# A ConvFFN whose weight-block sums move to VectorE, with reordered tile steps and an open last tile

## The chip, the cores and the metric

The kernel runs on one core of a Trainium2 chip. The metric is device time in microseconds (us), from the start to the end of one execution. Three runs of the kernel before gave 2868.24, 2868.50 and 2880.14 us; the median is 2868.5 us. A core has five engines, each with an instruction queue of its own that it works through in order: TensorE (PE in the profile; its weight loads are PEld), VectorE (DVE), ScalarE (ACT), GpSimd (POOL) and SyncE (SP), which here issues DMA transfers. Results of matmuls go to PSUM banks; everything else lies in SBUF.

## The reference

The program is a backbone of two layers on 1024 latent tokens and 256 context tokens, with a model width of 1024. Layer 0 mixes tokens by a Fourier transform and a gated unit, layer 1 by neighbourhood attention. Each layer ends in a ConvFFN, which is what the change is about:

```
def conv_ffn(h, w_up, conv_w, conv_b, w_down):
    a = h @ w_up                                  # w_up: 1024 x 5632
    gate, val = a[..., :D_FF], a[..., D_FF:]      # D_FF = 2816
    g = gate[t-1]*conv_w[0] + gate[t]*conv_w[1] + gate[t+1]*conv_w[2] + conv_b
    return (silu(g) * val) @ w_down               # w_down: 2816 x 1024
x = x + g2 * conv_ffn(modulate(x, ...), ...)      # latents, both layers
ctx = ctx + cg2 * conv_ffn(modulate(ctx, ...), ...)   # context, layer 0 only
```

Layer 1 is the last one, so its ConvFFN works on the latents alone, that of layer 0 on latents and context. All data is 32-bit; the kernel gets the accuracy by splitting an operand into a high part (a rounded copy, on ACT) and a low part (the difference, on DVE) and using three matmuls (high by high, high by low, low by high).

## The kernel before, in words

**Tiles and passes.** A ConvFFN runs two passes, one for each half of the tokens (L470 `run`). In a pass, a loop goes over 22 tiles of 128 gate and 128 value columns of `w_up`. In layer 1 a half is 2 x 256 or 2 x 258 tokens, in layer 0 it is 2 x 320 or 2 x 324.

**Products.** Each tile's up projection is a 2x2 block product (gate and value columns times the two parts of the token half, with the depth of 1024 cut in two) done in seven products instead of eight, in the manner of Strassen and Winograd. The weights' operands are the blocks A00, A01, A11 and the sums S1 to S4: `S1 = A10 + A11` ("s", L270), `S3 = A00 - A10` (L279), `S2 = S1 - A00` (L280), `S4 = A01 - S2` (L283). The tokens' operands are B00, B10, B11 and the sums T1, T2, T3, N4. Products P1 to P7 are 12 matmuls each (L352). P6, P7, P4 and P3 continue in PSUM banks of earlier products, so between two of them the running sum is copied out: "c00" after P1, "U" after P6, "V" after P7, "c10" after P4, all copies on ACT (L366). The adds "c00+", "c11+", "c01+" are on DVE (L363).

**The weights' way.** `load0` and `load1` (L265) bring two blocks of 512 KB each into the two `wr` buffers, by SP. A `wr` buffer is free for the next load only when the low part of the last operand made from it is done. POOL makes the four sums; ACT makes the high parts (L273), DVE the low parts (L277). S3, S2 and S4 overwrite the raw blocks, so low A00 comes before S3 and S2, and low S1 before S4.

**The rest of a tile.** "gate" (L370, ACT) and "taps" (L377 and L379, DVE) are the convolution; then "silu" (L397, ACT), "mul" (L398, DVE), and the split of the result into `act`: "acth" (L384, ACT) and "actl" (L388, DVE). In the token lists a minus sign marks a step that belongs to the tile before. Down projection steps D0 to D3 (L428) use two finished tiles each, and their results are taken into the residual by X0 to X3 (L420, DVE). "prep" fetches a block of `w_down` (L295) and splits an earlier one (L550 on ACT, L551 on DVE). "N" runs one step of the `ahead` generator, which in pass 0 prepares the token operands of pass 1 on DVE and ACT and sends them to a buffer in HBM.

**What sets the order.** The lists STEADY, START (tile 0 of pass 0), SECOND (tile 1) and TURN (between the passes) hold the steps of one tile in program order; every engine gets its own instructions in that order. A wait therefore holds up whatever stands behind it on the same engine.

**Ends and entries.** START is fed by `operands` (L222), which makes the seven token operands of half 0 for each of four depth blocks in turn, with subtractions at L246. At the end of pass 1 the down projection of the last six feed-forward tiles stands alone (L515 on): first output blocks 4 to 7 for tiles NF-4 and NF-3 with a take each, then for each half of the tokens all eight output blocks for the last two tiles. In layer 1 each finished block is transposed (L1806), copied (L1810) and sent out (L1813). The attention stage starts with transposes of `vt` (L1161), whose context part is copied by DVE (L1155).

Of the kernel before, what the change touches and what calls it, by code (L numbers as in the profile page):

```python
# [78 lines left out]
class Ffn:  # L79
# [89 lines left out]
    def ahead(self):  # L169
# [52 lines left out]
    def operands(self):  # L222
# [3 lines left out]
        n = h.n  # L226
        self.late = {}
        x = {j: (self.hf[j][:, :n], self.hf[j][:, n:2 * n], self.hf[j + 4][:, :n], self.hf[j + 4][:, n:2 * n]) for j in range(4)}

        def split(op, j, x):  # L230
            self.net.split(self.part(0, op, j, 0), self.part(0, op, j, 1), x)
        for j in range(4):
            for i, c in enumerate(h.kept):
                if j < 3:
                    nc.scalar.activation(self.halo[:, j::4, i], self.hfa[j][:, :, c:c + 4], AF.Copy)
                else:
                    for k in (j, j + 4):
                        nc.scalar.activation(self.halo[:, k, i], self.hf[k][:, c:c + 4], AF.Copy)
            split("B00", j, x[j][0])
        for op, i in (("B10", 2), ("B11", 3)):  # L240
            for j in range(4):
                split(op, j, x[j][i])
        for j in range(4):
            b00, b01, b10, b11 = x[j]
            for o, a, b in ((b00, b01, b00), (b01, b11, b01), (b11, b11, b00), (b10, b10, b11)):
                nc.vector.tensor_tensor(o, a, b, ALU.subtract)  # L246
            for op, o in (("T1", b00), ("T2", b11), ("T3", b01), ("N4", b10)):
                if op == "T1" and j < 2:
                    split(op, j, o)
                else:  # L250
                    self.late.setdefault(op, []).append(lambda op=op, j=j, o=o: split(op, j, o))


    def up_weights(self, f, slots):
# [4 lines left out]
        op = nc.gpsimd.tensor_tensor  # L259
# [55 lines left out]
    def up(self, s, f, norm):  # L315
# [154 lines left out]
    def run(self, hooks, beside, early, done):  # L470
# [59 lines left out]


class Net:
# [243 lines left out]
    def finish(self, mats, srcs, order, update, ffn, acc, square):  # L776
# [349 lines left out]
    def qkv(self, h, pool, ready, begun):  # L1126
# [24 lines left out]
        def vv(pr, pl, pc):  # L1151
# [3 lines left out]
            nc.vector.tensor_copy(vt[:, NL:], pc)  # L1155
# [345 lines left out]
    def run(self, out):  # L1501
# [179 lines left out]
        with pool(name="psb", bufs=2, space=PSUM) as self.ps:  # L1681
# [32 lines left out]
            def done(d, b):  # L1714
                o, c = room(d, b), 0
# [3 lines left out]
                if 0 < d < KD - 1:  # L1719
# [49 lines left out]
        with pool(name="psd", bufs=2, space=PSUM, reuse_waits="tile") as self.ps, pool(name="ffn1", bufs=1) as fp:  # L1769
# [51 lines left out]
            def done(d, b):  # L1821
                if d > 0:
                    emit(d - 1, *((384, 256), (640, 384))[b])
                if d == KD - 1:
# [69 lines left out]
```

## Time and profile before

| What | Value |
| --- | --- |
| Median of three runs | 2868.5 us |
| The profiled execution's own time | 2875.23 us |
| Span in the profile | 2873.4 us |
| Busy: PE, DVE, ACT, POOL | 2759.1, 2241.9, 1399.4, 774.7 us |
| ConvFFN of layer 0, pass 0 and pass 1 | about 486 to 960, and 960 to 1370 us |
| qkv and attention | about 1392 to 2030 us |
| ConvFFN of layer 1, pass 0 and pass 1 | about 2098 to 2505, and 2505 to 2850 us |

The stage bounds are read from the first and last instructions of the lines of a stage. A row of a timeline gives the start of an instruction, its duration, the engine, the line and what it reads and writes; the bracket at the end is the idle time of the engine before it, and what ended that. A row of groups gives busy time, the mean of one in ns, and the sum of the idle times before them. A row of windows gives, for a stretch of time, the busy time of PE, PEld, DVE, ACT and POOL, then the clock granted to TensorE (1.00 is full speed), the share of the DMA engines and GB/s.

### The profile page before, as it was taken

What the parts mean: (1) busy time and instruction counts of PE and PEld (TensorE: products, weight loads), DVE (VectorE), ACT (ScalarE), POOL (GpSimd) and SP (SyncE); (2) the same over time, 40 slices, a digit from 0 to 9 for tenths busy, and PEclk for the clock granted to TensorE, in tenths of its full rate; (3) what the DMA queues carried; (4) which work ended last, traced back from release to release, by engine and by line L of the source; (5) the groups of instructions that cost most, each with busy time, mean ns of one, the idle gap of its engine ahead of it and who ended that gap; (6) DMA issues with size and microseconds to landing.
All of it is one profiled execution on the core that took longest, in us unless ns stands there. A gap on an engine that the chain in (4) does not pass through costs nothing.

```text
span 2873.4 us, 47178 instructions
## 1 busy us (share of the span) xinstructions
PE 2759.1 (96%) x17980; PEld 2516.1 (88%) x17980; DVE 2241.9 (78%) x3746; ACT 1399.4 (49%) x2784; POOL 774.7 (27%) x704
## 2 busy tenths in 40 slices
PE   7999998999999999999899998999989999999999
PEld 4668877999999999999788887999778889899998
DVE  4233477899999888888775676998279999999996
ACT  4322314554445544444443335998255555555554
POOL 0600013232222332222211111444323333243331
PEclk9999999899999999999799999999989999999999
DMA  8764262223334222222043325774223333433333
GB/s 290 215 198 136 79 213 90 89 86 98 96 96 146 83 81 82 81 81 82 14 139 140 131 102 165 182 179 113 59 59 103 113 107 105 133 98 105 92 104 96
DMA packets 347291, 334.79 MB, mean 117 GB/s; under 512 B 14825, under 2 KB 280121, under 8 KB 347065
## 3 DMA queue, kind: packets, MB, share of 16 engines
q1 hardware_dynamic: 342917, 322.85, 37.5%
q0 software_dynamic: 3808, 7.87, 0.9%
q8 instruction: 142, 2.33, 0.3%
q10 hardware_dynamic: 340, 1.06, 0.1%
q14 instruction: 84, 0.69, 0.1%
HBM read 281.43 MB, written 50.29 MB: 115 GB/s over the span
## 4 chain that ended last, share of the span: by engine, by line
PE 64%; DVE 21%; ACT 6%; issue 4%; DMA 3%; POOL 0%; SPq 0%; POOLq 0%; DVEq 0%; ACTq 0%
PE pq L352 19%; PE pq L581 15%; PE pq L428 11%; PE ps L581 6%; DVE xl L420 4%; DVE wh L277 3%; DVE wq L277 3%; DVE wd L551 3%; PE pq L669 2%; PE ps L590 2%; DVE g L377 2%; DVE g L398 2%; DMA wd<-in_ada_w_dram 1%; ACT g L370 1%; PE st L1305 1%
## 5 line engine op out<-in xcount | busy, mean ns | idle before, releaser
L428 PE MATMUL pq<-act,wd 128*128 128x320 f32 (+3 forms) x3696 | 611.0, 317 | 5.6 <-ACT act L384 4.9
L352 PE MATMUL pq<-hs,wh 128*128 128x320 f32 (+3 forms) x4128 | 599.0, 298 | 11.3 <-ACT hx L366 7.4
L352 PEld LDWEIGHTS pq<-hs,wh 128*128 128x128 f32 x4128 | 573.2, 190 | 17.7 <-ACT hx L366 9.4
L428 PEld LDWEIGHTS pq<-act,wd 128*128 128x128 f32 x3696 | 548.6, 190 | 25.6 <-ACT act L384 5.4
L352 PE MATMUL pq<-hs,wq 128*128 128x320 f32 (+3 forms) x3144 | 477.1, 301 | 37.6 <-ACT hx L366 34.7
L352 PEld LDWEIGHTS pq<-hs,wq 128*128 128x128 f32 x3144 | 441.7, 191 | 52.1 <-ACT hx L366 46.6
L581 PE MATMUL pq<-hs,wh 128*128 128x512 f32 (+3 forms) x2100 | 469.0, 358 | 3.3 <-DVE hs L823 3.3
L581 PEld LDWEIGHTS pq<-hs,wh 128*128 128x128 f32 x2100 | 365.8, 192 | 77.4 <-issue 6.2
L270 POOL TENSOR_TENSOR ws<-wr 128x512 f32<-128x512 f32 x88 | 131.6, 1496 | 734.0 <-DMA wr<-in_ffn_w_up_dram 537.9
L420 DVE SCALAR_TENSOR_TENSOR xl<-pq,mod,xl 128x320 f32<-128x320 f32 (+5 forms) x604 | 288.7, 510 | 15.1 <-PE pq L428 15.1
L366 ACT ACTIVATE hx<-pq 128x320 f32<-128x320 f32 (+3 forms) x352 | 143.8, 409 | 301.1 <-PE pq L352 277.7
L277 DVE TENSOR_TENSOR wq<-wr,wq 128x512 fp32r<-128x512 f32 x262 | 240.5, 937 | 25.1 <-ACT wq L273 24.9
L581 PE MATMUL ps<-hs,wh 128*128 128x512 f32 x840 | 242.5, 408 | 4.2 <-ACT hs L820 1.7
L280 POOL TENSOR_TENSOR wr<-ws,wr 128x512 f32<-128x512 f32 x88 | 117.4, 1334 | 260.2 <-DVE wh L277 241.0
L581 PEld LDWEIGHTS ps<-hs,wh 128*128 128x128 f32 x840 | 143.4, 193 | 42.8 <-issue 14.4
L273 ACT ACTIVATE wh<-ws 128x512 fp32r<-128x512 f32 x172 | 108.0, 628 | 148.2 <-PE pq L352 145.3
L277 DVE TENSOR_TENSOR wh<-ws,wh 128x512 fp32r<-128x512 f32 x172 | 157.3, 914 | 21.7 <-ACT wh L273 19.3
L273 ACT ACTIVATE wq<-wr 128x512 fp32r<-128x512 f32 x262 | 162.9, 622 | 17.8 <-POOL wr L279 11.6
L1105 DVE RECIPROCAL hsq<-hsq 128x512 f32<-128x512 f32 (+1 forms) x40 | 121.1, 3030 | 52.8 <-ACT hsq L1104 51.9
L363 DVE TENSOR_TENSOR hx<-hx,pq 128x320 f32<-128x320 f32 (+3 forms) x266 | 118.6, 446 | 42.2 <-PE pq L352 26.0
L551 DVE TENSOR_TENSOR wd<-wrd,wd 128x512 fp32r<-128x512 f32 x176 | 142.6, 849 | 0.0
L279 POOL TENSOR_TENSOR wr<-wr,wr 128x512 f32<-128x512 f32 x88 | 135.7, 1542 | 6.9
(321 smaller groups left out, 4229.1 us busy)
## 6 DMA issues: line engine op xcount, KB each, us to landing
wr<-in_ffn_w_up_dram SPq DMA_DIRECT2D x176, 512.0 KB, 4.5
wrd<-in_ffn_w_down_dram SPq DMA_DIRECT2D x88, 512.0 KB, 3.6
adaw<-in_ada_w_dram SPq DMA_DIRECT2D x128, 256.0 KB, 3.6
wd<-in_ada_w_dram SPq DMA_DIRECT2D x32, 512.0 KB, 4.7
wr<-in_odd_w_qkv_dram SPq DMA_DIRECT2D x24, 512.0 KB, 4.2
vd<-kvs SPq DMA_DIRECT2D x8, 1280.0 KB, 7.3
v<-vd SPq DMA_DIRECT2D x16, 640.0 KB
kd<-kvs SPq DMA_DIRECT2D x8, 1280.0 KB, 4.6
```

Of the source, the lines that this page charges most:

```text
L270: op(raw["S1"], raw["A10"], raw["A11"], ALU.add)
L273: nc.scalar.activation(slots[name][:, 0], raw[name], AF.Copy)
L277: nc.vector.tensor_tensor(slots[name][:, 1], x, f32(slots[name][:, 0]), ALU.subtract)
L279: op(raw["A10"], x, raw["A10"], ALU.subtract)
L352: nc.tensor.matmul(o, w[wn][:, wp, k], self.part(s, bn, k, sp), start=(onto is None and k == 0 and i == 0), stop=(k == 3 and i == 2), skip ...
L363: return lambda: nc.vector.tensor_tensor(x[o], x[a], x[b], ALU.add)
L366: return lambda: nc.scalar.activation(x[o], x[a], AF.Copy)
L420: nc.vector.scalar_tensor_tensor(x, pd[:, a - lo:b - lo], net.mod[:, self.layer, st, 5, d:d + 1], x, ALU.mult, ALU.add)
L428: self.nc.tensor.matmul(pd, self.wds[j][i][:, wp, d % 4], self.acts[f][:, sp, lo:lo + m], start=(first and pi == 0), stop=(last and pi == 2))
L551: return (e or self.nc.vector).tensor_tensor(l, src, f32(h), ALU.subtract)
L581: nc.tensor.matmul(o, w(wp, k), s(k, sp), start=(ki == 0 and pi == 0), stop=(ki == len(order) - 1 and pi == 2))
L1105: nc.vector.reciprocal(r, r)
```

## The change

The change has five parts.

1. The four sums of weight blocks of each tile are made by VectorE instead of GpSimd (the one line in `up_weights`).
2. In STEADY the copy "U" stands ahead of "acth-", "prep" comes after "mul-" instead of ahead of P2, and "N" stands in the list twice, with `ahead` cut into smaller steps.
3. The entry (START, SECOND and `operands`) makes the token operands one operand at a time and not one depth block at a time, and its products come in another order (P1+ and P2+, the second depth halves, ahead of P3).
4. At the end of pass 1, output blocks 4 to 7 of tiles NF-4 and NF-3 stay open in eight PSUM banks and are finished with the last two tiles, so that they are taken once and not twice. The blocks then come in the order 4, 5, 6, 7, 0, 1, 2, 3, and one early transposed output stands behind every second of them.
5. The context part of `vt` is copied by ACT, and the last pair of heads has its products in the order k, q, v.

```
-    STEADY = ("P1", "X2-", "prep", "P2", "c00", "silu-", "mul-", "hA00", "P6", "acth-", "c00+", "actl-", "P5", "U", "hA01",
+    STEADY = ("P1", "X2-", "P2", "c00", "silu-", "mul-", "prep", "hA00", "P6", "c00+", "U", "acth-", "P5", "actl-", "hA01",
               "lA00", "X3-", "P7", "hS1", "lS1", "D0", "V", "c11+", "lA01", "P4", "hS2", "hS3", "X0", "lS2", "D1", "c10",
-              "lS3", "load0", "hA11", "P3", "lA11", "load1", "X1", "N", "D2", "hS4", "c01+", "gate", "lS4", "taps", "D3", "s")
+              "lS3", "N", "load0", "hA11", "P3", "lA11", "load1", "X1", "N", "D2", "hS4", "c01+", "gate", "lS4", "taps", "D3", "s")
-    START = ("P1", "first", "hA00", "lA00", "oT1", "P2", "c00", "hA01", "lA01", "c00+", "P3", "oT2", "sums", "P1+", "oT3",
-             "hS1", "lS1", "c00++", "P2+", "c00p+", "P5", "oN4", "hS2", "lS2", "prep", "P6", "U", "load0", "c01+", "P7", "V",
-             "c11+", "hS3", "lS3", "c01p5", "P4", "c10", "hA11", "lA11", "gate", "load1", "hS4", "taps", "lS4", "s")
-    SECOND = ("P6", "silu-", "hA00", "U", "mul-", "P5", "acth-", "hA01", "lA00", "actl-", "P7", "hS1", "lS1", "V", "c11+",
+    START = ("P1", "first", "hA00", "lA00", "oB11", "P2", "c00", "hA01", "lA01", "c00+", "P1+", "dT1", "oT1", "P2+", "dT3",
+             "sums", "P3", "dT2", "oT2", "c00++", "P5", "oT3", "hS1", "lS1", "P6", "U", "c00p+", "c01+", "dN4", "oN4",
+             "P7", "V", "hS2", "lS2", "c11+", "load0", "hS3", "lS3", "c01p5", "P4", "c10", "gate", "hA11", "lA11", "taps",
+             "load1", "hS4", "prep", "lS4", "s")
+    SECOND = ("P6", "U", "silu-", "hA00", "mul-", "P5", "acth-", "hA01", "lA00", "actl-", "P7", "hS1", "lS1", "V", "c11+",
...
     def up_weights(self, f, slots):
-        op = nc.gpsimd.tensor_tensor
+        op = nc.vector.tensor_tensor
...
     def run(self, hooks, beside, early, done):
...
-        side = early()
-        for d in range(4, KD):
-            self.down(1, NF - 3, d)
-            next(side, None)
-        self.prep(NF)
+        side, out = early(), {}
+        for i in range(2):
+            for d in range(4, KD):
+                if i == 0:
+                    out[d] = self.outs(1)
+                self.down_part(NF - 3, i, d, out[d], i == 0, False)
+                if d % 2:
+                    next(side, None)
+            self.down_weights(NF - 1, (i,))
         for b, block in enumerate(self.blocks(1)):
-            for d in range(KD):
-                self.down(1, NF - 2 + d // 4, d, [block])
-                if d == 0:
+            for n, d in enumerate((4, 5, 6, 7, 0, 1, 2, 3)):
+                if d < 4:
+                    self.down(1, NF - 2, d, [block])
+                else:
+                    for i in range(2):
+                        self.down_part(NF - 1, i, d, out[d][b:b + 1], False, i == 1)
+                    self.take(1, d, out[d][b:b + 1])
+                if n == 0:
                     for _ in side:
                         pass
-                done(d, b)
+                done(n, d, b)
...
-            nc.vector.tensor_copy(vt[:, NL:], pc)
+            nc.scalar.activation(vt[:, NL:], pc, AF.Copy)
...
-            for which in range(3):
+            for which in (1, 0, 2) if pr == NPAIR - 1 else range(3):
```

The first place is VectorE in a steady tile of layer 1, pass 1, from the last low parts of one tile's weights (`wq`) to the product by the value columns (`g<-g,hx`). `xl` rows are takes, the two rows with `cols` are the taps, `wd` rows are the low parts of `w_down`. Before:

```order
L277 TENSOR_TENSOR wq_20845<-wr_27941,wq_20845 128x512
L420 SCALAR_TENSOR_TENSOR xl_3681<-pq_28108,mod_127,xl_3681 128x256
L420 SCALAR_TENSOR_TENSOR xl_3681<-pq_28115,mod_127,xl_3681 128x258
L363 TENSOR_TENSOR hx_27982<-hx_27982,pq_28039 128x258
L277 TENSOR_TENSOR wh_20648<-ws_27980,wh_20648 128x512
L377 SCALAR_TENSOR_TENSOR g_28160<-hx_27982,cols_175_786,g_28160 128x515
L379 SCALAR_TENSOR_TENSOR g_28160<-hx_27982,cols_175_786,g_28160 128x515
L420 SCALAR_TENSOR_TENSOR xl_3783<-pq_28144,mod_127,xl_3783 128x256
L420 SCALAR_TENSOR_TENSOR xl_3783<-pq_28151,mod_127,xl_3783 128x258
L551 TENSOR_TENSOR wd_28197<-wrd_28004,wd_28197 128x512
L551 TENSOR_TENSOR wd_28200<-wrd_28004,wd_28200 128x512
L398 TENSOR_TENSOR g_28160<-g_28160,hx_27982 128x516
```

After (the line numbers are those of the changed kernel):

```order
L284 TENSOR_TENSOR wq_20797<-wr_27921,wq_20797 128x512
L428 SCALAR_TENSOR_TENSOR xl_3681<-pq_28088,mod_127,xl_3681 128x256
L428 SCALAR_TENSOR_TENSOR xl_3681<-pq_28095,mod_127,xl_3681 128x258
L371 TENSOR_TENSOR hx_27962<-hx_27962,pq_28019 128x258
L284 TENSOR_TENSOR wh_20628<-ws_27960,wh_20628 128x512
L385 SCALAR_TENSOR_TENSOR g_28140<-hx_27962,cols_175_786,g_28140 128x515
L387 SCALAR_TENSOR_TENSOR g_28140<-hx_27962,cols_175_786,g_28140 128x515
L277 TENSOR_TENSOR ws_28159<-wr_28120 128x512
L428 SCALAR_TENSOR_TENSOR xl_3783<-pq_28124,mod_127,xl_3783 128x256
L428 SCALAR_TENSOR_TENSOR xl_3783<-pq_28131,mod_127,xl_3783 128x258
L406 TENSOR_TENSOR g_28140<-g_28140,hx_27962 128x516
L568 TENSOR_TENSOR wd_28193<-wrd_28000,wd_28193 128x512
```

The sum S1 (`ws<-wr`) now stands on VectorE behind the taps and ahead of two takes and of the product `g<-g,hx`, which has moved ahead of the `wd` rows. The transfer that S1 reads is issued when the first row of the piece is done.

The second place is ScalarE in the same tile: from the gate (`g<-hx,cols,cols`) to the high part of `act`. `hx<-pq` rows are the copies c00 and U, `wh` rows are high parts of weights. Before:

```order
L370 ACTIVATE g_27563<-hx_27385,cols_31_139,cols_175_786 128x516
L550 ACTIVATE wd_27600<-wrd_27407 128x512
L550 ACTIVATE wd_27603<-wrd_27407 128x512
L366 ACTIVATE hx_27584<-pq_27585 128x258
L397 ACTIVATE g_27563<-g_27563 128x516
L273 ACTIVATE wh_20647<-wr_27527 128x512
L384 ACTIVATE act_27637<-g_27563 128x516
L366 ACTIVATE hx_27584<-pq_27585 128x258
```

After:

```order
L378 ACTIVATE g_27543<-hx_27365,cols_31_139,cols_175_786 128x516
L374 ACTIVATE hx_27564<-pq_27565 128x258
L405 ACTIVATE g_27543<-g_27543 128x516
L567 ACTIVATE wd_27596<-wrd_27403 128x512
L567 ACTIVATE wd_27599<-wrd_27403 128x512
L280 ACTIVATE wh_20627<-wr_27507 128x512
L374 ACTIVATE hx_27564<-pq_27565 128x258
L392 ACTIVATE act_27619<-g_27543 128x516
```

U is now ahead of the high part of `act`, which waits for VectorE's product, and the two `wd` rows are behind silu.

The third place is VectorE at the entry of layer 0's ConvFFN, from its first low part of weights (`wd<-wr`). `act`, `g` and `wq` rows of 128x320 are token blocks, `hs` rows the low parts of token operands. Before:

```order
L277 TENSOR_TENSOR wd_4144<-wr_3814,wd_4144 128x512
L277 TENSOR_TENSOR wh_3835<-wr_4128,wh_3835 128x512
L246 TENSOR_TENSOR act_3138<-act_3138 128x320
L551 TENSOR_TENSOR hs_2897<-act_3138,hs_2896 128x320
L246 TENSOR_TENSOR g_3833<-wq_3834,g_3833 128x320
L551 TENSOR_TENSOR hs_2921<-act_3138,hs_2920 128x320
L246 TENSOR_TENSOR act_3139<-act_3139 128x320
L551 TENSOR_TENSOR hs_2903<-act_3139,hs_2902 128x320
```

After:

```order
L284 TENSOR_TENSOR wd_4116<-wr_3814,wd_4116 128x512
L277 TENSOR_TENSOR ws_4121<-wr_4119 128x512
L284 TENSOR_TENSOR wh_3835<-wr_4100,wh_3835 128x512
L286 TENSOR_TENSOR wr_4119<-wr_4100,wr_4119 128x512
L287 TENSOR_TENSOR wr_4100<-ws_4121,wr_4100 128x512
L568 TENSOR_TENSOR hs_2897<-act_3138,hs_2896 128x320
L568 TENSOR_TENSOR hs_2903<-act_3139,hs_2902 128x320
L568 TENSOR_TENSOR hs_2909<-act_3140,hs_2908 128x320
```

Three sums stand ahead of the token operands on VectorE, the first of them right behind the low part whose buffer the transfer for it needs; the operands then follow one operand at a time.

More of the change, by code (lines that the diff above doesn't have):

```diff
@@ L200, in ahead @@
                                 nc.scalar.activation(o, o, AF.Identity, bias=sh[:, k:k + 1])
+                    if k < 4:
+                        yield
+                        if m == h.n:
+                            yield
                 to = self.nd[:, j, :, q * m:(q + 1) * m]
@@ L204, in ahead @@
                 yield
-                for o, x, y in ((b00, b01, b00), (b01, b11, b01), (b11, b11, b00), (b10, b10, b11)):
+                if m == h.n:
+                    yield
+                for i, (o, x, y) in enumerate(((b00, b01, b00), (b01, b11, b01), (b11, b11, b00), (b10, b10, b11))):
                     nc.vector.tensor_tensor(o, x, y, ALU.subtract)
+                    if i == 1:
+                        yield
+                        if m == h.n:
+                            yield
                 for i, x in enumerate(tmp):
@@ L209, in ahead @@
                 yield
+                if m == h.n:
+                    yield
     def bring(self, op):
@@ L220, in parted, with operands @@
             self.net.split(hi, lo, f32(lo))
-    def operands(self):
+    def operands(self, i):
         nc = self.nc
         h = self.halves[0]
-        n = h.n
-        self.late = {}
+        n, c = h.n, h.kept[i]
         x = {j: (self.hf[j][:, :n], self.hf[j][:, n:2 * n], self.hf[j + 4][:, :n], self.hf[j + 4][:, n:2 * n]) for j in range(4)}
-        def split(op, j, x):
-            self.net.split(self.part(0, op, j, 0), self.part(0, op, j, 1), x)
         for j in range(4):
[L233 to L240, printed above, removed]
-            for j in range(4):
[L242 to L251, printed above, removed]
@@ new lines, in operands, with split, sub @@
+            if j < 3:
+                nc.scalar.activation(self.halo[:, j::4, i], self.hfa[j][:, :, c:c + 4], AF.Copy)
+            else:
+                for k in (j, j + 4):
+                    nc.scalar.activation(self.halo[:, k, i], self.hf[k][:, c:c + 4], AF.Copy)
+        def split(op, b):
+            for j in range(4):
+                self.net.split(self.part(0, op, j, 0), self.part(0, op, j, 1), x[j][b])
+        def sub(o, a, b):
+            for j in range(4):
+                nc.vector.tensor_tensor(x[j][o], x[j][a], x[j][b], ALU.subtract)
@@ L358, in first @@
             w["A11"] = self.t([P, 2, 4, P], "wd", F32R, 4)
-            for st in (now["A11"], soon["load1"], soon["s"]):
-                st()
+            now["A11"]()
+            soon["load1"]()
+            soon["s"]()
         def add(o, a, b):
@@ L488, in run @@
                         ops, nxt = self.up(0, 0, none), None
-                        for k, fns in self.late.items():
-                            ops["o" + k] = lambda fns=fns: [fn() for fn in fns]
+                        ops.update(self.late)
                         ops["sums"] = hooks[1]
@@ L796, in rest @@
                     self.spread_to(acc(b)[0], cols[b])
-                ffn.first_norm(b // 2)
+                if b == 0:
+                    ffn.first_norm(0)
+                    ffn.operands(0)
                 if b == seq[-2]:
-                    ffn.operands()
+                    ffn.late["oB00"]()
+                    ffn.late["oB10"]()
+                if b == 2:
+                    ffn.first_norm(1)
+                    ffn.operands(1)
             if b == seq[-1]:
@@ L1712, in run, with done @@
                     [((xl, 0, 508, 324, 60),), ((xl, 0, 832, 192, 64), (xc, 1, 0, NCX, 256))])
-            def done(d, b):
-                o, c = room(d, b), 0
+            def done(k, d, b):
+                o, c = room(k, b), 0
                 for x, t0, n in late[0][b]:
@@ L1819, in early, with done @@
                     yield
[L1821 to L1824, printed above, removed]
+            last = []
+            def done(n, d, b):
+                if n > 0:
+                    emit(last.pop(), *((384, 256), (640, 384))[b])
+                if n == KD - 1:
                     emit(d, *((384, 256), (640, 384))[b])
+                else:
+                    last.append(d)
             ffn.run(hooks, iter(()), early, done)
```

7 lines of the change are left out of this document (6 added, 1 removed).

## The prediction

> **What bounds the kernel now.** I read the page first: busy time, then the chain.
>
> ```profile
> PE 2759.1 (96%) x17980; PEld 2516.1 (88%) x17980; DVE 2241.9 (78%) x3746; ACT 1399.4 (49%) x2784; POOL 774.7 (27%) x704
> ...
> PE 64%; DVE 21%; ACT 6%; issue 4%; DMA 3%; POOL 0%; SPq 0%; POOLq 0%; DVEq 0%; ACTq 0%
> ```
>
> PE is nearly full over the whole span, yet a fifth of the chain lies on DVE. So the bound changes from stage to stage. The view of windows, by stage, says where:
>
> ```profile
> 2157.80:2354.40 196.60, 180.88 (x1200) 165.60 (x1200) 184.54 (x253) 98.99 (x202) 62.39 (x44) 0.97 0.36 107
> 2354.40:2464.60 110.20, 110.06 (x760) 102.17 (x759) 105.39 (x141) 59.97 (x113) 40.30 (x28) 1.00 0.34 101
> 2538.10:2828.60 290.50, 289.69 (x2376) 286.52 (x2375) 278.04 (x433) 152.18 (x289) 104.55 (x72) 1.00 0.33 98
> 520.00:960.00 440.00, 427.79 (x2869) 424.07 (x2868) 404.06 (x742) 219.58 (x436) 122.98 (x88) 0.99 0.34 100
> 973.00:1370.00 397.00, 396.51 (x2675) 395.97 (x2675) 340.19 (x599) 190.57 (x333) 112.52 (x84) 1.00 0.28 82
> ```
>
> The rows are: layer 1, pass 0, its 11 tiles that also prepare pass 1; its 7 tiles that no longer do; pass 1, 18 tiles; layer 0, pass 0 and pass 1. Per tile the first three are 17.87, 15.74 and 16.14 us long, with 16.8, 15.1 and 15.4 us of DVE. Layer 1 is thus a close race: PE wins in rows 2 and 3 by 0.7 us, DVE in row 1, where PE idles 15.7 us and loses clock (0.97). Layer 0's pass 1 is PE's alone, with 57 us of free DVE.
>
> What fills DVE? One steady tile of pass 1 in the timeline (DVE, then POOL, then SP):
>
> ```profile
> 2703.79 1.78 DVE L398 TENSOR_TENSOR g<-g,hx 128x516 f32<-128x516 f32 x1
> 2710.13 1.73 DVE L277 TENSOR_TENSOR wq<-wr,wq 128x512 fp32r<-128x512 f32 x1
> 2712.57 0.68 DVE L277 TENSOR_TENSOR wh<-wr,wh 128x512 fp32r<-128x512 f32 x1
> 2713.17 1.28 DVE L277 TENSOR_TENSOR wq<-wr,wq 128x512 fp32r<-128x512 f32 x2
> 2714.38 0.87 DVE L420 SCALAR_TENSOR_TENSOR xl<-pq,mod,xl 128x256 f32<-128x256 f32 x2
> 2717.26 0.76 DVE L379 SCALAR_TENSOR_TENSOR g<-hx,cols,g 128x515 f32<-128x515 f32 x1
> 2717.93 0.87 DVE L420 SCALAR_TENSOR_TENSOR xl<-pq,mod,xl 128x256 f32<-128x256 f32 x2
> ...
> 2703.68 1.33 POOL L270 TENSOR_TENSOR ws<-wr 128x512 f32<-128x512 f32 x1 [8.50 <-DMA wr<-in_ffn_w_up_dram]
> 2710.02 1.29 POOL L283 TENSOR_TENSOR ws<-wr 128x512 f32<-128x512 f32 x1 [0.69 <-DVE wh L277]
> ...
> 2698.35 0.37 SPq L265 DMA_DIRECT2D wr<-in_ffn_w_up_dram  x1
> 2713.32 1.53 SPq L265 DMA_DIRECT2D wr<-in_ffn_w_up_dram  x2
> ```
>
> The same low part (L277) takes 0.68 us at 2712.57 and 1.73 us at 2710.13, where POOL's S4 has just begun. The mul at 2703.79 does likewise beside S1. Takes, which read PSUM, keep their 0.87 us. The groups of DVE over the whole of pass 1 (2520 to 2850 us) show the sum:
>
> ```profile
> L277 DVE TENSOR_TENSOR wq<-wr,wq 128x512 fp32r<-128x512 f32 x60 | 59.6, 1019 | 0.0
> L277 DVE TENSOR_TENSOR wh<-ws,wh 128x512 fp32r<-128x512 f32 x39 | 38.5, 988 | 0.1
> L398 DVE TENSOR_TENSOR g<-g,hx 128x516 f32<-128x516 f32 x21 | 31.9, 1521 | 0.0
> L277 DVE TENSOR_TENSOR wh<-wr,wh 128x512 fp32r<-128x512 f32 x39 | 30.9, 793 | 0.1
> L388 DVE TENSOR_TENSOR act<-g,act 128x516 fp32r<-128x516 f32 x20 | 19.4, 970 | 7.4 <-ACT act L384 7.4
> ```
>
> Above 0.68 us each these are 20.3, 12.0, 17.7, 4.4 and 5.8 us: 60 us over some 20 tiles, so **3.0 us per tile** that DVE loses to POOL's sums.
>
> **The change, part by part.**
>
> *Sums on DVE.* Four instructions of the size of L277: 0.60 us (start to start, 2712.57 to 2713.17) to 0.68 each, so 2.4 to 2.7 us per tile, against the 3.0 us of stalls that go. DVE's work comes out 0.3 to 0.6 us shorter: pass 1 15.45 - 3.0 + 2.4 = 14.85 us. The Trainium skill has the mechanism (SBUF — State Buffer, Who interferes with whom): a VectorE instruction with two SBUF inputs and a GpSimd instruction that reads SBUF exclude each other for the whole instruction. The 1.73 against 0.68 agrees.
>
> But DVE now waits where POOL waited. S1 reads what load1 brings. Load1 leaves SP when the last low part is done (2714.45, the end of the row at 2713.17; the second issue of SP's row follows). In the quoted tile POOL's S1 began at 2703.68, 5.33 us after the issue at 2698.35. DVE reaches S1's place behind the taps at 2717.93, 3.5 us after that low part. So DVE will stand for about 1.8 us, less what POOL needs to wake (not shown; 0 to 0.4 us), with two takes and the mul queued behind. Nothing hides it. Pass 1's DVE cycle is 14.85 + 0.3 (the idle time ahead of the taps) + 1.4 to 1.8 = 16.5 to 17.0, against PE's 16.14. I take 16.6, since some wake time is likely: +0.45 us over 20 tiles, **+9 us** (0 if the transfer lands 0.5 us earlier, +16 at the upper end).
>
> *STEADY order.* In layer 1's pass 0 the gaps have one form (ACT, PE, then DVE):
>
> ```profile
> 2217.84 0.63 ACT L384 ACTIVATE act<-g 128x512 fp32r<-128x512 f32 x1 [3.43 <-DVE g L398]
> 2218.38 0.37 ACT L366 ACTIVATE hx<-pq 128x256 f32<-128x256 f32 x1
> ...
> 2218.79 1.71 PE L352 MATMUL pq<-hs,wq 128*128 128x256 f32 x12 [2.41 <-ACT hx L366]
> ...
> 2213.74 2.39 DVE L551 TENSOR_TENSOR wd<-wrd,wd 128x512 fp32r<-128x512 f32 x2
> 2216.05 1.75 DVE L398 TENSOR_TENSOR g<-g,hx 128x512 f32<-128x512 f32 x1
> ```
>
> P7 waits for copy U, U for acth on ACT, acth for the mul, and the mul for two `wd` rows and POOL's lock (1.75). With U first, that chain is cut. The groups of PE in pass 0 of layer 0 (510 to 960) and of layer 1 (2098 to 2500) carry it:
>
> ```profile
> L352 PE MATMUL pq<-hs,wq 128*128 128x320 f32 (+1 forms) x792 | 131.2, 315 | 11.6 <-ACT hx L366 11.5
> ...
> L352 PE MATMUL pq<-hs,wq 128*128 128x256 f32 (+1 forms) x792 | 113.0, 293 | 23.5 <-ACT hx L366 21.0 <-DVE hs L551 2.1
> ```
>
> Layer 1: the 18 tiles last 306.8 us. Their DVE work is 289.9 us; 3.0 less and 2.4 more each leave 279, 15.5 per tile. With 0.3 ahead of the taps and the wait at S1, partly filled by the finer `ahead` steps (the second N stands between load1 and S1), I get 16.0 to 17.0. I take 16.5, 297 us: **-10** (-23 if PE sets every tile at 15.74, +3 at 17.0 and a late transfer). Layer 0, pass 0: DVE has 404 of 440 us and PE idles 12.2; half of it goes, **-6** (-3 to -9). Pass 1: 0, since DVE's free 57 us cover the wait.
>
> The Trainium skill (TensorE: Matmul & The Clock Gate, HAM oscillation) sets the limit for keeping the clock at gaps of 3.4 us. Here the clock falls to 0.97 in a row whose quoted gap is 2.41, so gaps below that figure do cost; by the rule the -10 would lose about 5.
>
> *Entry, ends, attention.* Four rows of PE's timeline:
>
> ```profile
> 525.05 2.23 PE L352 MATMUL pq<-hs,wq 128*128 128x320 f32 x7 [3.48 <-ACT hx L366]
> ...
> 1759.77 0.63 PE L1161 MATMUL pq<-ident,vt 128*128 128x128 f32 x2 [1.94 <-DVE vt L1155]
> ...
> 1377.61 6.67 PE L428 MATMUL pq<-act,wd 128*128 128x324 f32 x33 [2.88 <-ACT act L384]
> ...
> 2850.87 0.50 PE L428 MATMUL pq<-act,wd 128*128 128x258 f32 x2 [2.02 <-ACT act L384]
> ```
>
> Layer 0's entry: U ahead of silu removes 3.5 us, and the slow clock after it perhaps 2; DVE's wait for load1 at tile 1's S1 (ahead of all token operands; the load can't leave before the low part just ahead) gives 2 back: **-3.5** (-7 to +2). Layer 1's entry has the same gaps, with no quoted row: -3 by the first. Its turn between the passes, likewise by U: -3. Layer 0's tail: eight products of open blocks fill the 2.88 us, and some of the slow clock behind it: **-4** (0 to -6). Attention: the copy leaves DVE, where it ended last, and the last pair's v comes with no other work behind it; 1.94 plus clock: **-5** (-8 to 0). Layer 1's tail: its gap of 2.02 goes, and four pairs of takes with it, but more of the transposed outputs now come behind the last products and share four output buffers; I take **+3** (-2 to +6).
>
> The sum: +9 - 10 - 6 - 3.5 - 3 - 3 - 4 - 5 + 3 = **-22.5 us**. The profiled execution lasted 2875.2 us, 6.7 above the median of the three runs; 2852.7 for it is 2846 for a median run.
>
> **The rivals.**
>
> *No change.* U was not the cause but the next in line: DVE sets layer 1's pass 0 either way, the gap returns at another copy, and the pass gains 4 instead of 10; pass 1 loses 12, the tail 6. Sum -22.5 + 6 + 3 + 3 = -10.5, so 2858, inside the 0.5% (14 us) that a measurement of this kernel can tell from nothing. For it: DVE at 94% of row 1. Against: the chain named above ends at the lock, which goes.
>
> *Slower.* One mechanism: DVE's in-order wait at S1. In pass 0 the transfers share the queue with those of `ahead` (DMA share 0.36 against 0.33), so load1 lands 2 us later than the 5.33; every tile of layer 1 is then 15.5 + 0.3 + 3 = 18.8 long in pass 0, +31 instead of -10, and pass 1 +16. Sum -22.5 + 41 + 7 = +25: 2894; with half the delay +5 to +10. It decides once the wait passes 1.3 us in pass 0 (17.04 - 15.8, its mean now). Against it: the `ahead` steps behind load1 fill part of the wait. In the Trainium skill, Perfetto Trace Analysis (Optimizing Scalar/DVE Operations) goes this way: when VectorE is saturated, move work off it, even to GpSimd. Row 1 is such a place; the same page warns that the two share a port, and 1.73 against 0.68 bears out the warning more.
>
> *Larger gain.* The transfer lands in time, and PE sets all tiles: pass 0 -23, pass 1 0, tail 0: -22.5 - 13 - 9 - 3 = -47.5, so 2821. For it: POOL's wake time in the 5.33. Against: 1.8 us is a long wake time.
>
> **How the numbers follow.** Chances: forecast 0.47, no change 0.24, larger gain 0.15, slower 0.14. The forecast's own range is 2832 to 2858. Leaving 1 in 10 out at each side, the range is 2818 to 2872. Faster by over 0.5% (below 2854) takes 0.43 of the forecast's 0.47, the larger gain and 0.02 of no change: 0.60. Slower by over 0.5% (above 2883) is 0.12 of the slower case. The rest is 0.28.
>
> **What would show it.** L284 (the low parts) at 0.68 throughout and the mul at 0.69: the lock is gone. DVE idle ahead of S1 (L277 of the changed kernel) ended by the DMA of `w_up`, 1.4 to 1.8 us in layer 1: the new wait; its absence means the larger gain. Tiles of 16.5 in both passes of layer 1. No gap at P7 behind U. PE's gaps at 525, 1377 and 1759 shorter, and a last stretch of layer 1 that ends on output transfers. Tiles of 17 and more, with POOL gone, would make me wrong.

## The result, and the profile after

The changed kernel is **slower**: 2900.39 us median of four runs (2896.26 to 2906.42), against 2869.67 us for four runs of the kernel before. The ratio is 1.0094, with a 95% interval of 1.0072 to 1.0117. Forecast were 2846 us and a range of 2818 to 2872. The profiled execution has a span of 2894.5 us, against 2873.4 before: 21.1 us more. The times here and below are of runs with a granted clock of 0.97 and more; one run, of the version with S1 later, took 3788.49 us at a granted clock of 0.65 and is left out of its median.

Busy time and the chain, from the page of the changed kernel:

```profile
PE 2755.2 (95%) x17980; PEld 2506.8 (87%) x17980; DVE 2206.1 (76%) x4070; ACT 1392.5 (48%) x2792; POOL 275.9 (10%) x352
...
PE 64%; DVE 19%; DMA 10%; issue 4%; ACT 3%; SPq 0%; POOL 0%; DVEq 0%; ACTq 0%; POOLq 0%
```

DVE's work did fall, by 36 us, although it got 324 instructions more. But the chain now has 10% of DMA, where it had 3%. The view of waits of DVE puts a name to it:

```profile
DVE ws L277 <- DMA wr<-in_ffn_w_up_dram: 101.1, 71, 4.2
```

DVE stood 101.1 us at S1 (L277 of the changed kernel), 71 times, up to 4.2 us each. The groups of DVE in layer 1's pass 1 (2545 to 2850 us) show both sides of the trade:

```profile
L284 DVE TENSOR_TENSOR wq<-wr,wq 128x512 fp32r<-128x512 f32 x54 | 35.5, 686 | 0.0
L284 DVE TENSOR_TENSOR wh<-ws,wh 128x512 fp32r<-128x512 f32 x36 | 24.6, 684 | 0.0
L406 DVE TENSOR_TENSOR g<-g,hx 128x516 f32<-128x516 f32 x18 | 12.3, 686 | 0.0
L277 DVE TENSOR_TENSOR ws<-wr 128x512 f32<-128x512 f32 x18 | 12.5, 693 | 30.2 <-DMA wr<-in_ffn_w_up_dram 30.2
```

The low parts (1019 and 988 ns before) and the mul (1521) are all at 686 ns: the lock is gone. The price is in the last row, 30.2 us of idle time over 18 tiles, 1.68 us each.

The windows that answer to the five rows before, for layer 1 between the same tiles (layer 1's pass 0 with and without preparing work, its pass 1; the two rows of layer 0 are stretches of time and not of tiles):

```profile
2159.40:2345.50 186.10, 178.01 (x1203) 160.64 (x1203) 167.76 (x287) 96.50 (x195) 0.00 (x0) 1.00 0.35 107
2345.50:2462.90 117.40, 111.12 (x753) 100.31 (x752) 105.05 (x179) 59.86 (x118) 0.00 (x0) 1.00 0.35 105
2544.70:2851.30 306.60, 293.29 (x2380) 287.68 (x2380) 269.36 (x505) 152.25 (x288) 0.00 (x0) 1.00 0.30 93
520.00:960.00 440.00, 426.63 (x2851) 423.15 (x2851) 396.69 (x824) 214.01 (x429) 0.00 (x0) 0.98 0.34 100
973.00:1375.00 402.00, 399.68 (x2695) 398.86 (x2695) 350.38 (x679) 190.40 (x339) 9.49 (x6) 1.00 0.27 82
```

Pass 1 of layer 1 took 306.6 us for 18 tiles (17.03 each) and had 290.5. Here is where the 21 us came from, as stages between the gates of the same tiles in both profiles:

| Stage | Before | After | Difference |
| --- | --- | --- | --- |
| Entry of layer 0 (first three tiles) | 53.8 | 56.2 | +2.4 |
| Layer 0, pass 0, steady tiles | 336.7 | 332.3 | -4.4 |
| Layer 0, turn and first tiles of pass 1 | 142.6 | 152.2 | +9.6 |
| Layer 0, rest of pass 1 | 317.0 | 314.5 | -2.6 |
| Layer 0's tail, qkv, attention | 757.8 | 752.0 | -5.8 |
| Entry of layer 1 (two tiles) | 31.0 | 33.2 | +2.2 |
| Layer 1, pass 0, 16 tiles | 275.3 | 271.2 | -4.1 |
| Layer 1, turn | 105.0 | 114.2 | +9.2 |
| Layer 1, pass 1, 18 tiles | 290.5 | 306.6 | +16.1 |
| Last tile and tail | 44.9 | 43.2 | -1.7 |

The wait in a steady tile of pass 1 (SP, then DVE):

```profile
2576.78 1.57 SPq L272 DMA_DIRECT2D wr<-in_ffn_w_up_dram  x2
...
2580.75 0.76 DVE L387 SCALAR_TENSOR_TENSOR g<-hx,cols,g 128x515 f32<-128x515 f32 x1
2583.06 0.69 DVE L277 TENSOR_TENSOR ws<-wr 128x512 f32<-128x512 f32 x1 [1.55 <-DMA wr<-in_ffn_w_up_dram]
```

The second of the two loads left at about 2577.9; S1 started 5.1 us later, and DVE had been free from 2581.5 on. In layer 1's turn it is worse (SP, then DVE):

```profile
2460.70 1.57 SPq L272 DMA_DIRECT2D wr<-in_ffn_w_up_dram  x2
2463.63 6.47 SPq L228 DMA_DIRECT2D hs<-nd  x10
...
2464.54 0.75 DVE L387 SCALAR_TENSOR_TENSOR g<-hx,cols,g 128x511 f32<-128x511 f32 x1
2468.51 0.69 DVE L277 TENSOR_TENSOR ws<-wr 128x512 f32<-128x512 f32 x1 [3.22 <-DMA wr<-in_ffn_w_up_dram]
```

There the operands of pass 1 (`hs<-nd`) come in just behind the weights, and S1 waits 3.22 us; over the six tiles of the turn DVE stood 13.7 us at S1. With the sums on POOL the same transfers ended idle time of POOL, which has 0% of the chain before. From the page of the kernel before:

```profile
L270 POOL TENSOR_TENSOR ws<-wr 128x512 f32<-128x512 f32 x88 | 131.6, 1496 | 734.0 <-DMA wr<-in_ffn_w_up_dram 537.9
```

### The profile page after: what moved, and what is told of

Read it like the earlier page. It is cut to its first block, busy times and chain, and to the rows that moved or that the text cites. A ratio compares the mean times of both kernels' runs of the same rounds, so it can differ in the third digit from the quotient of the medians.

```text
span 2894.5 us, 46551 instructions
## 1 busy us (share of the span) xinstructions
PE 2755.2 (95%) x17980; PEld 2506.8 (87%) x17980; DVE 2206.1 (76%) x4070; ACT 1392.5 (48%) x2792; POOL 275.9 (10%) x352
## 4 chain that ended last, share of the span: by engine, by line
PE 64%; DVE 19%; DMA 10%; issue 4%; ACT 3%; SPq 0%; POOL 0%; DVEq 0%; ACTq 0%; POOLq 0%
PE pq L359 18%; PE pq L598 15%; PE pq L436 11%; DMA wr<-in_ffn_w_up_dram 7%; PE ps L598 6%; DVE xl L428 3%; DVE wh L284 3%; DVE wq L284 2%; DVE wd L568 2%; PE pq L686 2%; PE ps L607 2%; PE st L1329 1%; PE tl L1362 1%; DVE hx L371 1%; DMA wd<-in_ada_w_dram 1%
## 5 line engine op out<-in xcount | busy, mean ns | idle before, releaser
L359 PE MATMUL pq<-hs,wh 128*128 128x320 f32 (+3 forms) x4128 | 606.3, 300 | 37.9 <-DVE hx L371 28.0
L359 PEld LDWEIGHTS pq<-hs,wq 128*128 128x128 f32 x3144 | 439.5, 190 | 33.6 <-ACT hx L374 30.2
L428 DVE SCALAR_TENSOR_TENSOR xl<-pq,mod,xl 128x320 f32<-128x320 f32 (+3 forms) x588 | 282.3, 516 | 10.8 <-PE pq L436 10.8
L284 DVE TENSOR_TENSOR wq<-wr,wq 128x512 fp32r<-128x512 f32 x262 | 176.1, 694 | 14.4 <-ACT wq L280 14.4
L280 ACT ACTIVATE wh<-wr 128x512 fp32r<-128x512 f32 x172 | 107.3, 624 | 108.1 <-DVE wr L287 107.2
L277 DVE TENSOR_TENSOR ws<-wr 128x512 f32<-128x512 f32 x88 | 60.8, 691 | 101.1 <-DMA wr<-in_ffn_w_up_dram 101.1
L284 DVE TENSOR_TENSOR wh<-ws,wh 128x512 fp32r<-128x512 f32 x172 | 119.3, 693 | 13.8 <-ACT wh L280 13.7
L378 ACT ACTIVATE g<-hx,cols,cols 128x640 f32<-128x640 f32 (+3 forms) x88 | 76.5, 869 | 105.8 <-DVE hx L371 105.7
L284 DVE TENSOR_TENSOR wh<-wr,wh 128x512 fp32r<-128x512 f32 x172 | 119.7, 696 | 0.0
```

What stands on the lines that cost most here:

```text
L277: op(raw["S1"], raw["A10"], raw["A11"], ALU.add)
L280: nc.scalar.activation(slots[name][:, 0], raw[name], AF.Copy)
L284: nc.vector.tensor_tensor(slots[name][:, 1], x, f32(slots[name][:, 0]), ALU.subtract)
L359: nc.tensor.matmul(o, w[wn][:, wp, k], self.part(s, bn, k, sp), start=(onto is None and k == 0 and i == 0), stop=(k == 3 and i == 2), skip ...
L378: nc.scalar.activation(x["g"], x["C0"], AF.Identity, bias=net.convb[:, layer * NF + f:layer * NF + f + 1], scale=cw[:, NF + f:NF + f + 1])
L428: nc.vector.scalar_tensor_tensor(x, pd[:, a - lo:b - lo], net.mod[:, self.layer, st, 5, d:d + 1], x, ALU.mult, ALU.add)
```

## The experiments

Theory A: the loss is DVE standing in order at S1 until load1 lands. Theory B: the new orders (U, prep, entry, tail) lose it. A further rival: the sums' work itself is too much for DVE.

### Sums back on GpSimd, all else as changed

```
-        op = nc.vector.tensor_tensor
+        op = nc.gpsimd.tensor_tensor
```

> The changed kernel with its four sums back on GpSimd; the orders, entry, tail and copy stay as changed. Theory A (the loss is VectorE standing at S1 until load1 lands): in the changed kernel VectorE idled 101 us at S1, 30 us of it in layer 1's pass 1 and 20 us in the two turns; here that idle time is 0, layer 1's pass 1 goes back to tiles of 16.1 us, the two turns lose the 18 us that they gained, and the median is 2845 to 2862 us, faster than the kernel before. Theory B (the new orders are the loss, above all U, prep and the entry): the turns stay 8 us or more above before each and the median stays above 2880 us.

Measured: 2870.2 us against 2872.21, ratio 0.9992 (0.9978 to 1.0006). The median lies between what A and what B gave. The loss went, but the gain that A named did not come: without the moved sums, the other four parts can't be told from nothing together. Layer 1 in windows (pass 0 with and without preparing work, pass 1), then one row each of PE's and DVE's timelines, and one of DVE's groups (2149 to 2531 us):

```profile
2149.20:2338.40 189.20, 179.94 (x1212) 162.35 (x1211) 181.40 (x243) 94.64 (x196) 63.70 (x44) 1.00 0.35 106
2338.40:2456.10 117.70, 111.78 (x748) 100.42 (x748) 113.54 (x151) 58.25 (x119) 39.70 (x28) 1.00 0.35 105
2531.20:2823.80 292.60, 289.11 (x2381) 286.95 (x2380) 286.17 (x433) 147.79 (x288) 104.57 (x72) 1.00 0.33 97
...
2222.88 1.71 PE L359 MATMUL pq<-hs,wq 128*128 128x256 f32 x12 [0.35 <-ACT hx L374]
...
2238.96 3.47 DVE L568 TENSOR_TENSOR wd<-wrd,wd 128x512 fp32r<-128x512 f32 x2
...
L284 DVE TENSOR_TENSOR wq<-wr,wq 128x512 fp32r<-128x512 f32 x66 | 64.0, 996 | 0.0
```

The lock is back (996 ns), and has only found other victims: the two `wd` rows and the mul took 2.39 and 1.75 us in the tile that the prediction shows; with the mul ahead of prep they take 3.47 and 0.69. Layer 1's pass 0 needs 275.0 us for its 16 tiles, as before (275.3). The turns, with 147.6 and 107.0 us, lie 5.0 and 2.0 us above before; so of the change's 9.6 and 9.2 a part is the orders' (in layer 0 half of that comes back in the rest of pass 1, 293.1 + 21.4 us against 295.7 + 21.4) and the rest the wait's.

### Nothing but the engine of the sums

The kernel before, with the one line `op = nc.vector.tensor_tensor`.

> The kernel before with nothing changed but the engine of the four sums (VectorE instead of GpSimd). Theory A (wait at S1): slower than before by as much as the whole change or more, 2895 to 2920 us, with some 100 us of VectorE idle at S1 ended by the transfer of w_up. Theory B (the orders): within 10 us of before, 2860 to 2880 us.

Measured: 2923.05 us against 2872.21, ratio 1.0172 (1.0140 to 1.0203). Waits of DVE, and the same three windows:

```profile
DVE ws L270 <- DMA wr<-in_ffn_w_up_dram: 86.0, 49, 4.9
...
2164.80:2359.00 194.20, 179.05 (x1200) 164.38 (x1199) 172.85 (x297) 98.87 (x202) 0.00 (x0) 0.98 0.36 109
2359.00:2477.20 118.20, 110.90 (x758) 102.15 (x757) 101.56 (x169) 59.26 (x112) 0.00 (x0) 1.00 0.31 94
2563.70:2876.10 312.40, 292.86 (x2389) 289.54 (x2388) 271.29 (x505) 151.72 (x290) 0.00 (x0) 0.99 0.30 90
```

Theory A: one line costs 51 us, more than the whole change. With the other parts of the change the loss is smaller (2900 against 2923). DVE's work is smaller than before in every row, and every row but the first is longer.

### S1 alone back on GpSimd

```
-            op(raw["S1"], raw["A10"], raw["A11"], ALU.add)
+            nc.gpsimd.tensor_tensor(raw["S1"], raw["A10"], raw["A11"], ALU.add)
```

> The changed kernel with S1 alone on GpSimd, and S3, S2 and S4 still on VectorE. Theory A (it is the in-order wait for the transfer, not the work): VectorE no longer waits for load1; S2, the next that needs it, comes about 8.3 us after load1's issue, the transfer and S1 need 6.4 to 7.7, so 0 to 1 us of wait a tile is left; tiles of layer 1 fall to 15.8 to 16.3, median 2840 to 2855 us. Rival (the work of the sums itself is too much for VectorE): tiles of layer 1's pass 1 stay at 16.8 or more and the median above 2885 us.

Measured: 2854.92 us against 2872.21, ratio 0.9941 (0.9919 to 0.9962): the upper end of what A gave. Waits of DVE, and the windows:

```profile
DVE wr L286 <- POOL ws L277: 19.9, 5, 5.2
...
2154.50:2337.10 182.60, 177.60 (x1206) 161.41 (x1205) 173.32 (x276) 96.50 (x196) 16.20 (x11) 1.00 0.36 110
2337.10:2449.90 112.80, 110.14 (x752) 100.42 (x752) 108.30 (x172) 59.65 (x119) 10.15 (x7) 1.00 0.37 109
2521.40:2807.10 285.70, 285.70 (x2375) 285.57 (x2374) 274.70 (x487) 150.99 (x289) 28.86 (x18) 1.00 0.33 100
```

DVE does three of the four sums and still lets PE run at 100% in pass 1: the work was never too much. What is left of the wait (19.9 us in 5 places) comes at the entries and just ahead of them.

### All sums on VectorE, S1 later

The step "s" goes from the end of a tile's list into the next tile's list. A minus sign calls the step of the tile before.

```
-  ... "gate", "lS4", "taps", "D3", "s")
+  ... "gate", "lS4", "taps", "D3")
-  ... "actl-", "hA01", "lA00", "X3-", ...
+  ... "actl-", "hA01", "s-", "lA00", "X3-", ...
```

SECOND and START likewise; behind TURN the step is handed on (`ops["s"] = old["s"]`).

> The changed kernel with all four sums on VectorE, but the step s moved from the end of a tile's list to the next tile's list, just ahead of the low part of A00 (behind the product, the prep, c00+ and actl), in all lists; at the entry S1 of tile 1 stays where it was. Theory A (in-order wait): S1 comes about 7 us after load1's issue, the transfer needs 5.1 to 6.2, so the wait is gone but for the entries (about 18 us of idle there stay); tiles of layer 1 at 15.8 to 16.2, turns as before, median 2840 to 2855 us. Rival (VectorE's work is too much): no change against the changed kernel, above 2885 us.

Measured: 2845.26 us (the median of three) against 2872.21, ratio 0.9902 (0.9874 to 0.9930): theory A. Waits of DVE, and the windows:

```profile
DVE ws L277 <- DMA wr<-in_ffn_w_up_dram: 15.0, 4, 3.9
...
2149.00:2330.00 181.00, 178.67 (x1211) 161.73 (x1210) 169.00 (x288) 96.06 (x196) 0.00 (x0) 1.00 0.37 111
2330.00:2441.30 111.30, 110.20 (x752) 100.19 (x751) 105.71 (x179) 59.59 (x119) 0.00 (x0) 1.00 0.37 111
2513.40:2799.40 286.00, 286.00 (x2379) 286.00 (x2379) 270.61 (x505) 152.08 (x289) 0.00 (x0) 1.00 0.33 99
```

101.1 us of waiting became 15.0, with the same instructions on the same engines. Pass 1 has 15.89 us per tile.

### Tile 1's sums on GpSimd as well

```
-            self.soon = self.up_weights(1, self.slots)
+            self.soon = self.up_weights(1, self.slots, nc.gpsimd.tensor_tensor)
```

(`up_weights` takes the sums' operation as an argument; the step s is late, as above.)

> The kernel with s moved late, and beside it the four sums of tile 1 alone (the one whose S1 stands at the entry of each layer's ConvFFN) on GpSimd. Theory A (at the entry too it is VectorE's wait for load1 that PE feels): PE's gaps of 4.2 us at 494 and 4.9 us at 2099 go, the two entries are 5 to 9 us shorter together, median 2837 to 2842 us. Rival (the entry is bound by the token operands, the gap only moves): within 2 us of the kernel with s late, 2844 to 2848 us.

Measured: 2840.7 us against 2870.74, ratio 0.9897 (0.9873 to 0.9921). The median lies where A put it, but the stages do not bear A out: the entries are 54.4 and 30.4 us long, against 54.5 and 30.5 with S1 on DVE. Against their own runs of the kernel before, this version and the one before it are the same (0.9897 and 0.9902), and most of the 4.9 us between their profiles lies outside the ConvFFN, in stages that the edit doesn't touch. PE's gap of 4.2 us at 494 us went, and another grew. From the timelines of ACT and PE:

```profile
520.36 1.28 ACT L405 ACT_TABLE_LOAD   x1 [2.06 <-DVE g L387]
524.96 0.42 ACT L374 ACTIVATE hx<-pq 128x320 f32<-128x320 f32 x1
...
525.43 3.03 PE L359 MATMUL pq<-hs,wq 128*128 128x320 f32 x10 [4.71 <-ACT hx L374]
```

The copy that PE waits for 4.71 us is now V, the next copy after U: it stands on ACT behind silu, which has to wait for its table load of 1.28 us, and behind acth. So the rival holds at the entry: the gap only moves.

### S1 late, without any other part of the change

The kernel before, with the sums on VectorE and the step s late (the two edits above).

> The kernel before with the sums on VectorE and s late, and nothing else of the change (old U, prep, entry, tail, copy, head order). If the sums without a wait carry the gain by themselves: 2848 to 2856 us, tiles of layer 1's pass 1 at 15.9 us, and layer 1's pass 0 as short as with the new order. If U ahead of the high part of act matters too (the prediction's step): layer 1's pass 0 keeps gaps at P7 behind U and lies 5 us or more above that of the kernel with s late (261.8 us for its 16 tiles), and the median is 2856 to 2866 us.

Measured: 2838.68 us against 2870.74, ratio 0.9888 (0.9863 to 0.9913); in a second set (below) 2842.20 us, 0.9890 (0.9869 to 0.9910). Waits of DVE, and the windows:

```profile
DVE ws L270 <- DMA wr<-in_ffn_w_up_dram: 8.4, 3, 3.9
...
2142.90:2327.50 184.60, 176.88 (x1202) 162.06 (x1201) 171.97 (x298) 100.07 (x201) 0.00 (x0) 1.00 0.38 115
2327.50:2435.50 108.00, 108.00 (x754) 100.85 (x753) 101.70 (x169) 60.40 (x112) 0.00 (x0) 1.00 0.33 102
2506.40:2791.70 285.30, 285.30 (x2373) 285.30 (x2373) 270.58 (x505) 153.81 (x289) 0.00 (x0) 1.00 0.33 99
```

This pair with the second experiment is the cleanest of all: the same kernel, the same work on the same engines, one step moved in its list, 2923 against 2839 us. And with U, prep, N, entry, tail and copy as they were, layer 1's pass 0 (261.5 us for 16 tiles) is as short as with the new order (261.8). The entries, 52.4 and 28.0 us, are shorter by more than 2 us each than with the new lists (54.5 and 30.5, fourth experiment).

### The old order of heads

In the fifth experiment's kernel, `for which in range(3)` for the last pair too.

> The kernel with s late and tile 1's sums on GpSimd, but the last pair of heads in the old order q, k, v (the copy stays on ACT). In the changed kernel the attention starts 6.6 us after the last qkv product, in the kernel before 5.1 us, both behind a reciprocal of 3.35 us on VectorE. Theory (the new order lets that reciprocal stand ahead of the values' low part): 1 to 3 us shorter than with the order k, q, v. Rival (the order is worth what the prediction gave it): 2 to 4 us longer.

Measured: 2846.33 us against 2870.74, ratio 0.9904 (0.9870 to 0.9937); the new order has 0.9897 (0.9873 to 0.9921). The stage from layer 0's last gate to layer 1's first is 751.4 us, with the new order 751.3: neither theory shows in it. At the place itself the old order is shorter: PE's gap ahead of the first attention product is 1.99 us and not 4.66, but the next gap is 2.24 and not 0.57. Of the 9 us by which the two spans differ, 6.8 lie ahead of the first gate (522.8 against 516.0 us), where both are the same program.

### Only the new ends beside the late S1

The sixth experiment's kernel with part 4 of the change, and the sixth once more:

> The kernel before with the sums on VectorE and s late, and of the rest of the change only the ends of the ConvFFN (part 4, both layers). By the stages of the runs so far the new end is 4 to 7 us shorter in layer 0 and 3 to 4 us in layer 1, and the new entry is 2 us longer in each layer, so this has the one without the other: 2827 to 2835 us. Rival (the ends only shift time into the stages behind them): 2836 to 2842 us, as the same kernel with the old ends.

> The kernel before with the sums on VectorE and s late alone, once more beside the one with the new ends: 2836 to 2842 us by either theory; the difference between the two is the price of part 4.

Measured: 2839.39 us, ratio 0.9886 (0.9866 to 0.9905), and 2842.20 us, ratio 0.9890 (0.9869 to 0.9910), both against 2876.85. The intervals are almost the same, so the rival holds: the new ends can't be told from none. The last tile and tail are 46.0 us with them and 46.6 and 46.7 without; from layer 0's last gate to layer 1's first, the same kernel without them took 755.9 us in one profile and 749.9 in another, with them 754.4. Stages of this length can't be read to better than 6 us from single profiles, so the -5.8 of that row in the table above is not a shown gain, and the 0.1 us of the seventh experiment is no proof that the order of heads is worth nothing.

## Why the prediction was wrong

The sum was -22.5 us and the profiles differ by +21.1, so 44 us are to be found.

**Sums on DVE.** The lock and its size were right: in pass 1 of layer 1, 3.0 us per tile went and 2.5 came. That DVE would stand at S1 was right too, and in pass 1 even the size (1.4 to 1.8 forecast, 1.68 measured). Of that range the value near the lower end was taken, for POOL's time to wake; there was none to subtract: over the 18 tiles S1 started 5.20 us after the issue of load1 on DVE, and 5.14 us after it on POOL in the kernel before. DVE also had 15.0 us of work, not 14.85. So pass 1 came to +16.1 instead of +9, the upper end that was given (7 us of the 44). The lock that the Trainium skill states (SBUF — State Buffer, Who interferes with whom) shows in both directions: the low parts `wq` take 0.686 us without POOL's sums, and 0.996 with the sums back on it.

**The step that failed: outside the steady tiles DVE's wait for load1 was put at nothing, or too low.** For layer 1's turn the prediction had -3 "by U" and no wait. For layer 0's pass 1, turn included, it had 0, since "DVE's free 57 us cover the wait"; but the wait fell in the tiles of the turn, and the free time lay in the others. Layer 1's turn measured +9.2 us (12 us of the 44), and layer 0's turn and pass 1 +7.0 (7 us). DVE's groups in the changed kernel, over layer 1's pass 0 (16 tiles), layer 1's turn and layer 0's turn, in the bounds of the table:

```profile
L277 DVE TENSOR_TENSOR ws<-wr 128x512 f32<-128x512 f32 x16 | 11.1, 692 | 16.7 <-DMA wr<-in_ffn_w_up_dram 16.7
...
L277 DVE TENSOR_TENSOR ws<-wr 128x512 f32<-128x512 f32 x6 | 4.2, 692 | 13.7 <-DMA wr<-in_ffn_w_up_dram 13.7
...
L277 DVE TENSOR_TENSOR ws<-wr 128x512 f32<-128x512 f32 x7 | 4.8, 690 | 7.3 <-DMA wr<-in_ffn_w_up_dram 7.3
```

In layer 1's turn the wait is 2.3 us a tile. With S1 late and all else alike (the fourth experiment) the turns have 102.6 and 145.8 us instead of 114.2 and 152.2, so the wait cost 11.6 and 6.4 us there. The 3.2 us by which layer 0's turn stays above the kernel before are not the wait's: with the old lists and S1 late it has 141.4. In two tiles of layer 1's turn load1 shares the queue with the operands of pass 1: S1 starts 6.6 and 5.7 us after the issue, and DVE waits 3.22 and 3.50 us. That is the mechanism of the rival "slower" (a load that lands later), at another place than the steady tiles where that rival put it. It got 0.14. That its 2894 us lie near the measured 2900 is luck: it had +31 us in pass 0, where -4.1 was measured.

In layer 1's pass 0 the wait had been priced, as one that the finer `ahead` steps fill in part, and they did: 1.04 us a tile, against 1.68 in pass 1. Still the tiles came to 16.95 us, inside the 16.0 to 17.0 that were given and above the 16.5 that was taken, so the pass gained 4.1 us and not 10 (6 us of the 44); with S1 late it has 261.8 us, 13.5 below the kernel before. The entries came to +4.6 where -6.5 was forecast (11 us). Of this the wait is 4.4 us, the 56.2 and 33.2 us against 54.5 and 30.5 with S1 late; the prediction had 2, at layer 0's entry only. The other stages nearly cancel.

**U ahead of acth.** The chain P7, U, acth, mul, wd was there as described, and it did get cut: with the new order and POOL's sums, the gap at 2222.88 us in the same place is 0.35 us. But pass 0 gained nothing by it (275.0 against 275.3), and without it the late S1 gained as much (261.5). What set pass 0 was DVE's time, lock included: DVE is busy for 96% of its first row with the new order and POOL's sums, and the same order with the sums on DVE and S1 late has 261.8 us. A chain that PE waits on shows which instruction came last, not what its cutting is worth while another engine is as full. The rival "no change" said so, and for the order alone it holds.

**Entry.** U ahead of silu moved the gap to V, so its 3.5 us did not come. The new entry as a whole (lists and order of the operands, not tried apart) is more than 2 us longer in each layer than the old, measured with S1 late in both: the term was wrong in sign.

**Attention.** The copy left DVE, but something longer stays on it. From DVE's and PE's timelines of the changed kernel:

```profile
1755.24 3.35 DVE L1128 RECIPROCAL hsq<-hsq 128x512 f32<-128x512 f32 x1 [1.74 <-ACT hsq L1127]
1759.06 1.61 DVE L1190 TENSOR_TENSOR kvs<-pq,kvs 128x512 fp32r<-128x512 f32 x3
...
1760.39 0.58 PE L1329 MATMUL st<-k,q 128*128 128x256 f32 x1 [4.66 <-DVE kvs L1190]
```

The values' low parts queue behind the reciprocal of 3.35 us, so in place of PE's gaps of 0.83, 1.94 and 0.56 us there are now 0.60 and 4.66: 1.9 us more, where 5 fewer were forecast. Whether the stage as a whole got shorter is not shown; the two tails (-4 and +3) are too small to be told by these runs.

**What was right.** Layer 0's pass 0 gained 4.4 us (-6 forecast) and its steady pass 1 lost nothing, since DVE had time to spare there. Layer 1's tail came to -1.7, inside its bounds of -2 to +6.

**Left open.** Why the one-line change alone loses 51 us and the whole change 31, when DVE's idle time at S1 is 86.0 in the first and 101.1 in the second, was not tried part by part. Of the 27 us between the two profiles 19 lie in layer 1's pass 0, turn and pass 1 (278.4, 120.5 and 312.3 us against 271.2, 114.2 and 306.6), although DVE's idle time at S1 is the same there (59.4 and 60.6 us). The order of mul and prep is one candidate: the mul ahead of prep is not held up by it once DVE comes out of the wait late. That is argued, not shown.

**The better version.** Sums on VectorE with s late, and nothing else of the change, beats both kernels: 2838.68 and 2842.20 us in two sets, 1.1% below the kernel before.

## What to carry to other kernels

Before work is moved to an engine that runs in order, look not only at the work but at what the old engine waited for: the 538 us of POOL's idle time that the transfers ended delayed nothing on the chain, and the same transfers cost 101 us in front of everything on DVE. Such a move needs its instruction put at the place where its input is surely there, and that place has to be checked in the exceptional tiles (turns, entries), where other transfers share the queue. And cutting a chain was worth nothing in layer 1's pass 0 as long as another engine's total time set the stage.

## What the runs showed of the hardware

Two things had not been expected. First, the tile of 16.14 us that was read as PE's own time in layer 1's pass 1, with PE busy 289.7 of 290.5 us, was not its limit: with POOL quiet it is 15.85 us, and with S1 alone on POOL 15.87, at the same granted clock of 1.00. The groups of PE over 16 tiles of each, of the kernel before and of the sixth experiment:

```profile
L352 PE MATMUL pq<-hs,wq 128*128 128x258 f32 x576 | 78.8, 286 | 0.3 <-ACT hx L366 0.2
```

```profile
L352 PE MATMUL pq<-hs,wq 128*128 128x258 f32 x576 | 77.4, 283 | 0.0
```

The same 576 matmuls read 78.8 and 77.4 us, so what the profile shows as busy held some 2% that was not the matmuls' own, and 99.7% busy was not a floor. What PE stalled on is not shown.

Second, the lock between DVE and POOL is not bound to an instruction. The groups of the mul and of the `wd` rows over the 18 tiles of layer 1's pass 1, of the kernel before and then of the first experiment, where the mul stands ahead of prep:

```profile
L398 DVE TENSOR_TENSOR g<-g,hx 128x516 f32<-128x516 f32 x18 | 29.9, 1659 | 0.0
L551 DVE TENSOR_TENSOR wd<-wrd,wd 128x512 fp32r<-128x512 f32 x36 | 23.1, 683 | 0.0
...
L568 DVE TENSOR_TENSOR wd<-wrd,wd 128x512 fp32r<-128x512 f32 x36 | 40.8, 1175 | 0.0
L406 DVE TENSOR_TENSOR g<-g,hx 128x516 f32<-128x516 f32 x18 | 12.5, 697 | 0.2 <-ACT g L405 0.2
```

The mul lost 17.4 us, and the next instructions of that kind took on 17.7.
